# Two-layer diffusion trunk on one core: softmax weights split by ScalarE and VectorE straight from PSUM, q/k norm gains folded into the rotation tables, doubled heads written at once

## The chip, the core and the metric

The kernel runs on one core of a Trainium2 chip. The metric is the device time of one execution in microseconds, as the median over runs. Five engines work side by side, each through its own queue in order: TensorE (PE; PEld is its weight load), VectorE (DVE), ScalarE (ACT), GpSimd (POOL) and the queue from which the DMAs are issued (SP).

## The reference

Two token groups, 128 prompt tokens and 512 latent tokens, go through two layers with the same weights. What matters here is the attention part of a layer:

```
h  = rmsnorm(x, norm1) * (1 + sc1) + sh1
qa, ka, va, qb, kb, vb, uc = split(h @ w_in)
qa = rmsnorm(qa per head of 64, qn_a); ka, qb, kb alike with kn_a, qn_b, kn_b
if latent tokens: rotate qa, ka, qb, kb by cos, sin of the position; add the cached keys and values
oa: 4 heads, softmax(q1 k1 / 8) - lam * softmax(q2 k2 / 8), times va     (differential)
ob: 8 query heads over 2 key heads, softmax(q k / 8) times vb            (GQA)
oc: pooling mixer;  merged = gates * (oa, ob, oc projections);  x = x + g1 * (merged @ w_out)
```

A gated MLP follows. The normed keys (not rotated) and the values of the prompt tokens are outputs too.

## The kernel before

All tensors are float32. A matmul of full precision is made of three matmuls of fp32r operands: every operand is split into a high part (a copy rounded to fp32r) and a low part (the rest), and `mm3` adds high times low, low times high and high times high.

Each layer has an attention phase and then merge, out and MLP phases, which the change doesn't touch. The attention phase has six units in the order `order`: two GQA units (kind 1: 4 q heads and 1 k head) and four differential ones (kind 0: 2 q and 2 k heads). `unit` projects five token tiles of 128 (tile 0 is the prompt): 24 matmuls into one PSUM tile `mm` (`ps_m`, one slot), a copy to `raw` by ACT (two slots), then the norm and the rotation: `sqq` is the square by ACT, `ss` its sum per head and then mean plus eps by DVE, `rq` the power -1/2 by POOL (`powr`); `y0` is raw times the norm gain by POOL, `y` is y0 times cos by POOL, `y2` is y0 with its halves swapped times sin by two DVE instructions, POOL adds y2 to y, and two DVE instructions write y times rq into both halves of `dup`, in which each head stands twice. `transposes` turns dup on PE into `tr` (a PSUM tile), from which ACT writes the high part `qk` and DVE the low part.

A unit's attention (`tasks_gqa`, `tasks_diff`) runs while the next unit, or dense products of the pooling input (`in_u`), of gates (`gate`) and of the pooling mixer (`mix`), are projected; `weave` sets the order by cost figures, and the framework then orders instructions on each engine by a timeline of its own. Scores `sc` of 128 queries go through maximum (DVE), exponential (ACT) and scaling to the weights `w`. `pv_pair` turns the weights of two query tiles on PE into three PSUM tiles `pt` (512, 512 and 256 columns); `put_pt` splits each into `ph` and `pl`; the products with the values go to `pv`. In `put_pt` of before, ACT copies the PSUM tile to `pt` in SBUF, DVE casts that to ph, and POOL subtracts ph from it. `tr`, `pt` and `trc` (the cached keys) share a pool of two PSUM slots, `ps_t`. A PSUM slot is free again after its last reader.

GpSimd reads and writes SBUF alone here; all its instructions of the attention phase have SBUF operands.

Of the kernel before, what the change touches and what calls it, by code (L numbers as in the profile page):

```python
# [12 lines left out]
F32 = mybir.dt.float32  # L13
F32R = mybir.dt.float32r
AF = mybir.ActivationFunctionType
ALU = mybir.AluOpType
# [4 lines left out]
P = 128  # L21
# [7 lines left out]
EPS = 1e-6  # L29
# [27 lines left out]
def trunk_kernel(ctx: ExitStack, tc: tile.TileContext, a: dict):  # L57
    nc = tc.nc
    dma = nc.sync.dma_start
    vec, act, pool, pe = nc.vector, nc.scalar, nc.gpsimd, nc.tensor  # L60

    def tp(name, bufs=1, stack=None, **kw):
        return (stack or ctx).enter_context(
            tc.tile_pool(name=name, bufs=bufs, reuse_waits="tile", **kw))
# [173 lines left out]
    def attention_phase(l, hh, hl, w0):  # L238
        lam_init = 0.8 - 0.6 * math.exp(-0.3 * l)
        with ExitStack() as st:  # L240
            late = tp("late", 2, st)
            ap = tp("att", 2, st)
# [3 lines left out]
            rows = ap.tile([P, 8, 64], F32, tag="dup", name="rowv")  # L246
            dma(rows, a["rowv"][l])

            lt = ap.tile([P, 2, 64], F32, tag="sq", name="lt", bufs=5)
            lam2 = small.tile([P, 2], F32, tag="lam2", name="lam2", bufs=1)  # L250
            nlam = small.tile([P, 1], F32, tag="nlam", name="nlam", bufs=1)
            vec.tensor_tensor(out=lt[:, 0], in0=rows[:, 4], in1=rows[:, 5], op=ALU.mult)
# [3 lines left out]
            vec.tensor_tensor(out=nlam, in0=lam2[:, 1:2], in1=lam2[:, 0:1], op=ALU.subtract)  # L256
            vec.tensor_scalar_add(out=nlam, in0=nlam, scalar1=-lam_init)

            gains = []
            for kind, (nq, nk) in enumerate(((2, 2), (4, 1))):  # L260
                g = ap.tile([P, 5, 64], F32, tag=f"gain{kind}", name=f"gain{kind}", bufs=1)
                vec.tensor_scalar_mul(out=g[:, :nq], in0=rows[:, 2 * kind:2 * kind + 1].to_broadcast([P, nq, 64]),
                                      scalar1=0.125)
                vec.tensor_copy(g[:, nq:nq + nk], rows[:, 2 * kind + 1:2 * kind + 2].to_broadcast([P, nk, 64]))
                gains.append(g)
            cos = ap.tile([P, 4, 64], F32, tag="cos", name="cos", bufs=1)
            sin = ap.tile([P, 4, 64], F32, tag="sin", name="sin", bufs=1)
            dma(cos, a["cos"])
            dma(sin, a["sin"])
            subg = small.tile([P, 1], F32, tag="subg", name="subg", bufs=1)  # L270
            vec.tensor_scalar_mul(out=subg, in0=vecs[l][:, V_SL:V_SL + 1], scalar1=1.0 - lam_init)

# [18 lines left out]
            def unit(kind, idx, w, out, prefetch):  # L291

                nq, nk = (2, 2) if kind == 0 else (4, 1)
                nh = nq + nk
                g = gains[kind]
                vw = P if kind == 0 else 64
                qk = ap.tile([P, 6, 768], F32R, tag="qk", name="qk")
                v1 = ap.tile([P, 6, P], F32R, tag="v1", name="v1")
# [26 lines left out]
                ps = ps_t.tile([P, 4, P], F32, tag="p", name="trc")  # L325
                for i in range(nk):
# [3 lines left out]
                                  op=ALU.subtract)  # L330
# [4 lines left out]
                for tt in range(5):  # L335
                    ts = slice(tt * P, (tt + 1) * P)
                    ps = ps_m.tile([P, 384], F32, tag="mm", name="mm")
                    for k in range(ND):
                        hi, lo = w[k // 2]
                        ws = slice((k % 2) * 384, (k % 2) * 384 + 384)  # L340
                        mm3(ps, hh[:, k, ts], hl[:, k, ts], hi[:, ws], lo[:, ws], k == 0, k == 7)
                        yield 0.49
                    if late_tr is not None:
                        transposes(*late_tr)
                        yield 0.5
                    if tt == 3:
                        prefetch()
                    raw = ap.tile([P, 384], F32, tag="raw", name="raw")
                    act.activation(raw, ps, AF.Copy)  # L349
                    slot = 5 if tt == 0 else tt  # L350
                    put_v(raw[:, nh * 64:nh * 64 + vw], slot)
                    qkr = raw[:, :nh * 64].rearrange("p (h d) -> p h d", d=64)
                    sq = ap.tile([P, 5, 64], F32, tag="sq", name="sqq", bufs=5)
                    act.activation(sq[:, :nh], qkr, AF.Square)
                    ss = small.tile([P, 8], F32, tag="ss", name="ss")
                    vec.tensor_reduce(out=ss[:, :nh], in_=sq[:, :nh], axis=AX.X, op=ALU.add)
                    vec.tensor_scalar(out=ss[:, :nh], in0=ss[:, :nh], scalar1=1.0 / 64, scalar2=EPS,
                                      op0=ALU.mult, op1=ALU.add)
                    rr = small.tile([P, 8], F32, tag="rq", name="rq")
                    powr(rr[:, :nh], ss[:, :nh])  # L360
                    dup = ap.tile([P, 5, 2, 64], F32, tag="dup", name="dup")
                    y0 = ap.tile([P, 5, 64], F32, tag="sq", name="y0", bufs=5)
                    pool.tensor_tensor(out=y0[:, :nh], in0=qkr, in1=g[:, :nh], op=ALU.mult)
                    rb = rr[:, :nh].unsqueeze(2).to_broadcast([P, nh, 64])
                    if tt == 0:
                        for j in range(2):
                            vec.tensor_tensor(out=dup[:, :nh, j], in0=y0[:, :nh], in1=rb, op=ALU.mult)
# [6 lines left out]
                    else:  # L374
                        y = ap.tile([P, 5, 64], F32, tag="sq", name="y", bufs=5)
                        y2 = ap.tile([P, 5, 64], F32, tag="sq", name="y2", bufs=5)
                        pool.tensor_tensor(out=y[:, :nh], in0=y0[:, :nh],
                                           in1=cos[:, tt - 1:tt].to_broadcast([P, nh, 64]), op=ALU.mult)
                        for h in range(2):
                            hs = slice(32 * h, 32 * h + 32)  # L380
                            vec.tensor_tensor(out=y2[:, :nh, hs], in0=y0[:, :nh, 32 - 32 * h:64 - 32 * h],
                                              in1=sin[:, tt - 1:tt, hs].to_broadcast([P, nh, 32]), op=ALU.mult)
                        pool.tensor_tensor(out=y[:, :nh], in0=y[:, :nh], in1=y2[:, :nh], op=ALU.add)
                        for j in range(2):
                            vec.tensor_tensor(out=dup[:, :nh, j], in0=y[:, :nh], in1=rb, op=ALU.mult)
                    late_tr = (dup.rearrange("p h a d -> p h (a d)"), nh, nq, qk, slot)
                transposes(*late_tr)
                yield 0.5
# [50 lines left out]
            def put_pt(ps, n):  # L439
                ph = late.tile([P, 512], F32R, tag="ph", name="ph", bufs=3)  # L440
                pl = late.tile([P, 512], F32R, tag="pl", name="pl", bufs=2)
                st = late.tile([P, 512], F32, tag="pt", name="pt", bufs=2)[:, :n]
                act.activation(st, ps[:, :n], AF.Copy)
                vec.tensor_copy(ph[:, :n], st)  # L444
                pool.tensor_tensor(out=pl[:, :n], in0=st, in1=ph[:, :n].bitcast(F32), op=ALU.subtract)  # L445
                return ph, pl

            def pv_pair(ws, emit):
# [272 lines left out]
            for i, items in enumerate(FILL):  # L721
                made = []
                n = len(items)
# [5 lines left out]
                if i < len(order):  # L729
                    kind, idx = order[i]  # L730
# [162 lines left out]
    for c in range(2):  # L893
        ps = ps_d.tile("csp")
# [66 lines left out]
    for l in range(L):  # L961
        dst.close()
        xst.close()
        attention_phase(l, hh, hl, w0)
        w0 = None
        xst = ExitStack()
# [15 lines left out]
        with ExitStack() as ms:  # L982
# [11 lines left out]
            for gi, (f0, f1) in enumerate(GROUPS):  # L994
# [156 lines left out]
```

## Time and profile before

| what | value |
|---|---|
| median of 3 runs | 2333.85 us (2330.75 to 2335.5) |
| the profiled execution | 2329.09 us, span 2327.3 us |
| PE, DVE, ACT, POOL busy, share of the span | 96%, 70%, 42%, 32% |
| attention phase of layer 1 (first product of a unit to first gate of the merge phase) | 44.8 to 436.6 us |
| attention phase of layer 2 | 1183.2 to 1580.0 us |

The span runs from the first to the last instruction of the profile. A granted clock of 1.00 is 2.4 GHz on TensorE, 0.50 is 1.2 GHz. An engine's busy share is an average over very unlike stretches, so the rows further down are taken by stretch. A wait names the instruction that ended it.

### The profile page before, as it was taken

How to read it: one execution, taken by the hardware profiler on the slowest of the kernel's cores; microseconds unless marked ns; L12 is line 12 of the kernel's file. 1: busy time of each engine (PE TensorE's matmuls, PEld its weight loads, DVE VectorE, ACT ScalarE, POOL GpSimd, SP SyncE). 2: the span in 40 equal slices, each digit the busy share in tenths (PEclk: the TensorE clock that was granted, in tenths of full speed). 3: DMA queues.
4: the chain of work that ended last, by engine and by line, in shares of the span. 5: the costliest groups of instructions: out<-in, count | busy, mean ns of one | idle time of the engine just before them, and what ended most of it. 6: DMA issues, size and time to landing. Idle time of an engine off the chain costs nothing. (4 is left out here: it accounts for less than half of the span.)

```text
span 2327.3 us, 38124 instructions
## 1 busy us (share of the span) xinstructions
PE 2227.8 (96%) x14778; PEld 2168.6 (93%) x14778; DVE 1633.0 (70%) x2971; ACT 978.7 (42%) x1728; POOL 747.1 (32%) x835
## 2 busy tenths in 40 slices
PE   8988998999999999999988999999999999999999
PEld 4888988999999999999978988899999999999999
DVE  6888788559668757765598877965795776554555
ACT  4544555432245424332454545644323454242422
POOL 3886775215031000000058866642331300000000
PEclk8999999999999999999999999999999999999999
DMA  7211213276443333432232122224762422312123
GB/s 269 68 52 58 70 63 104 87 255 226 135 127 104 102 106 118 136 102 86 86 114 75 42 69 81 95 75 132 268 209 91 145 94 95 102 60 93 52 83 114
DMA packets 102776, 258.52 MB, mean 111 GB/s; under 512 B 19522, under 2 KB 32578, under 8 KB 102595
## 3 DMA queue, kind: packets, MB, share of 16 engines
q1 hardware_dynamic: 102596, 256.09, 33.7%
q8 instruction: 116, 1.90, 0.3%
q14 instruction: 64, 0.52, 0.1%
HBM read 233.10 MB, written 22.95 MB: 110 GB/s over the span
## 5 line engine op out<-in xcount | busy, mean ns | idle before, releaser
L96 DVE TENSOR_TENSOR wl<-st,wh 128x1024 fp32r<-128x1024 f32 (+3 forms) x336 | 388.7, 1161 | 75.5 <-ACT wh L95 74.6
L113 PE MATMUL up<-h2l,wh 128*128 128x320 f32 x1408 | 435.3, 310 | 2.4 <-DVE h2l L209 2.4
L95 ACT ACTIVATE wh<-st 128x1024 fp32r<-128x1024 f32 (+3 forms) x336 | 314.7, 943 | 291.0 <-PE dn L114 168.8
L114 PE MATMUL up<-h2h,wh 128*128 128x320 f32 x1408 | 434.9, 309 | 0.0
L112 PE MATMUL up<-h2h,wl 128*128 128x320 f32 x1408 | 432.8, 310 | 1.5 <-ACT v L851 1.4
L113 PEld LDWEIGHTS up<-h2l,wh 128*128 128x128 f32 x1408 | 264.8, 188 | 3.1 <-DVE h2l L209 3.1
L112 PEld LDWEIGHTS up<-h2h,wl 128*128 128x128 f32 x1408 | 264.0, 188 | 2.7 <-ACT v L851 1.9
L114 PEld LDWEIGHTS up<-h2h,wh 128*128 128x128 f32 x1408 | 264.8, 188 | 0.1
L143 DVE SCALAR_TENSOR_TENSOR junk<-stm,cs 128x1024 bf16<-128x1024 f32 x172 | 221.4, 1287 | 59.6 <-DMA stm<-in_w_mod 56.9
L445 POOL TENSOR_TENSOR pl<-pt,ph 128x512 fp32r<-128x512 f32 (+2 forms) x156 | 185.9, 1195 | 146.0 <-DVE ph L444 90.3
L854 DVE SCALAR_TENSOR_TENSOR v<-u,vecs,v 128x127 f32<-128x127 f32 (+1 forms) x176 | 89.0, 546 | 183.7 <-ACT v L851 183.7
L112 PE MATMUL mm<-wh,hl 128*128 128x384 f32 x480 | 169.6, 353 | 10.7 <-ACT raw L349 6.5
L113 PE MATMUL dn<-al,wh 128*128 128x320 f32 x544 | 168.1, 309 | 0.0
L114 PE MATMUL dn<-ah,wh 128*128 128x320 f32 x544 | 168.1, 309 | 0.0
L112 PE MATMUL dn<-ah,wl 128*128 128x320 f32 x544 | 168.1, 309 | 0.0
L113 PE MATMUL mm<-wl,hh 128*128 128x384 f32 x480 | 165.5, 345 | 1.5 <-DVE wl L96 1.5
L114 PE MATMUL mm<-wh,hh 128*128 128x384 f32 x480 | 164.7, 343 | 0.0
L125 POOL COPY stm<-v 128x1 f32<-128x1 f32 x32 | 27.6, 878 | 404.4 <-DVE v L856 339.8
L112 PE MATMUL gp<-hh,wl 128*128 128x320 f32 x480 | 148.4, 309 | 0.0
L114 PE MATMUL gp<-hh,wh 128*128 128x320 f32 x480 | 148.0, 308 | 0.0
L113 PE MATMUL gp<-hl,wh 128*128 128x320 f32 x480 | 148.0, 308 | 0.0
L112 PE MATMUL mmu<-hh,wl 128*128 128x384 f32 (+1 forms) x416 | 134.9, 324 | 7.1 <-ACT up L666 5.1
(227 smaller groups left out, 5787.1 us busy)
## 6 DMA issues: line engine op xcount, KB each, us to landing
stm<-in_w_mod SPq DMA_DIRECT2D x88, 512.0 KB, 4.3
st<-in_w_up SPq DMA_DIRECT2D x88, 512.0 KB, 3.6
st<-in_w_gate SPq DMA_DIRECT2D x48, 512.0 KB, 4.3
st<-in_w_unit SPq DMA_DIRECT2D x48, 384.0 KB, 3.3
st<-in_w_out SPq DMA_DIRECT2D x32, 512.0 KB, 3.7
st<-in_w_down SPq DMA_DIRECT2D x48, 320.0 KB, 2.9
st<-in_w_br SPq DMA_DIRECT2D x24, 512.0 KB, 3.6
st<-in_w_down SPq DMA_DIRECT2D x32, 384.0 KB, 3.2
```

The source lines that it names most:

```text
L95: act.activation(hi, x, AF.Copy)
L96: eng.tensor_tensor(out=lo, in0=x, in1=hi.bitcast(F32), op=ALU.subtract)
L112: pe.matmul(out, sl, mh, start=start, stop=False)
L113: pe.matmul(out, sh, ml, start=False, stop=False)
L114: pe.matmul(out, sh, mh, start=False, stop=stop)
L125: pool.tensor_copy(dst[:, 0:1], after[0])
L143: vec.scalar_tensor_tensor(out=junk, in0=st, scalar=1.0, in1=cs[:, j], op0=ALU.mult, op1=ALU.mult, accum_out=col)
L445: pool.tensor_tensor(out=pl[:, :n], in0=st, in1=ph[:, :n].bitcast(F32), op=ALU.subtract)
L854: vec.scalar_tensor_tensor(out=v[:, s + 1:e], in0=u[:, s:e - 1], scalar=cw[0], in1=v[:, s + 1:e], op0=ALU.mult, op1=ALU.add)
```

## The change

1. `put_pt`: ACT writes the high part `ph` straight from the PSUM tile, and DVE subtracts it from the same PSUM tile into `pl`. DVE's cast, POOL's subtraction and the SBUF tile `pt` are gone. The PSUM slot is now held until DVE's subtraction, and no longer until ACT's copy.
2. Norm gains: tables `cg` = gain times cos and `sg` = gain times sin are made once in a phase for each kind, for q and k apart. POOL makes `y` = raw times cg in one multiplication (two instructions in a GQA unit, 256 and 64 columns), DVE makes `y2` from raw and sg (two instructions, in a GQA unit four), so y0 is gone.
3. The square is scaled and a 65th column holds eps, so that the sum over it needs no further instruction (L357 of before is gone). The squares live in two tiles of their own.
4. One DVE instruction writes both halves of dup, for 4 or 5 heads 512 or 640 columns.
5. `cos` and `sin` are loaded into slots of the weight tiles `w`.

```diff
-            gains = []
...
+            vec.tensor_scalar_mul(out=rows[:, 0:4:2], in0=rows[:, 0:4:2], scalar1=0.125)
+            cos = late.tile([P, 4, 64], F32, tag="w", name="cos", bufs=4)
+            sin = late.tile([P, 4, 64], F32, tag="w", name="sin", bufs=4)
             dma(cos, a["cos"])
             dma(sin, a["sin"])
+            for kind in range(2):
...
+                for typ in range(2):
+                    g = rows[:, 2 * kind + typ:2 * kind + typ + 1]
+                    vec.tensor_copy(cg[:, 0:1, typ], g)
+                    vec.tensor_tensor(out=cg[:, 1:, typ], in0=cos, in1=g.to_broadcast([P, 4, 64]), op=ALU.mult)
+                    for h in range(2):
+                        hs, ho = slice(32 * h, 32 * h + 32), slice(32 - 32 * h, 64 - 32 * h)
+                        vec.tensor_tensor(out=sg[:, :, typ, hs], in0=sin[:, :, hs],
+                                          in1=g[:, :, ho].to_broadcast([P, 4, 32]), op=ALU.mult)
...
-                    act.activation(sq[:, :nh], qkr, AF.Square)
+                    act.activation(sq[:, :nh, :64], qkr, AF.Square, scale=0.125)
...
-                    vec.tensor_scalar(out=ss[:, :nh], in0=ss[:, :nh], scalar1=1.0 / 64, scalar2=EPS,
-                                      op0=ALU.mult, op1=ALU.add)
...
+                    for of, by in zip(parts, gain):
+                        pool.tensor_tensor(out=of(y), in0=of(qkr), in1=by(cg[:, tt]), op=ALU.mult)
                     powr(rr[:, :nh], ss[:, :nh])
-                    pool.tensor_tensor(out=y0[:, :nh], in0=qkr, in1=g[:, :nh], op=ALU.mult)
...
+                    vec.tensor_tensor(out=dup[:, :nh], in0=y[:, :nh].unsqueeze(2).to_broadcast([P, nh, 2, 64]),
+                                      in1=rr[:, :nh].unsqueeze(2).unsqueeze(2).to_broadcast([P, nh, 2, 64]),
+                                      op=ALU.mult)
...
-                        pool.tensor_tensor(out=y[:, :nh], in0=y0[:, :nh],
-                                           in1=cos[:, tt - 1:tt].to_broadcast([P, nh, 64]), op=ALU.mult)
...
-                        for j in range(2):
-                            vec.tensor_tensor(out=dup[:, :nh, j], in0=y[:, :nh], in1=rb, op=ALU.mult)
...
-                act.activation(st, ps[:, :n], AF.Copy)
-                vec.tensor_copy(ph[:, :n], st)
-                pool.tensor_tensor(out=pl[:, :n], in0=st, in1=ph[:, :n].bitcast(F32), op=ALU.subtract)
+                act.activation(ph[:, :n], ps[:, :n], AF.Copy)
+                vec.tensor_tensor(out=pl[:, :n], in0=ps[:, :n], in1=ph[:, :n].bitcast(F32), op=ALU.subtract)
```

In the kernel after, lines of this part stand 11 or 12 further down (L445 of before is L456).

POOL's queue in layer 1, where the attention of the first GQA unit runs beside the first `in_u` (the windowed sums are `win`). Before:

```order
L445 TENSOR_TENSOR pl<-pt,ph 128x256
L445 TENSOR_TENSOR pl<-pt,ph 128x512 x2
L673 TENSOR_TENSOR win<-up 128x663
L436 TENSOR_SCALAR w<-w,rs 128x640
L673 TENSOR_TENSOR win<-win 128x661
L436 TENSOR_SCALAR w<-w,rs 128x640
L673 TENSOR_TENSOR win<-win 128x657
L445 TENSOR_TENSOR pl<-pt,ph 128x256
L445 TENSOR_TENSOR pl<-pt,ph 128x512
L673 TENSOR_TENSOR win<-win 128x649
```

And now:

```order
L449 TENSOR_SCALAR w<-w,rs 128x640 x4
L684 TENSOR_TENSOR win<-up 128x663
L118 TENSOR_TENSOR rq<-ss,mhalf 128x4
L684 TENSOR_TENSOR win<-win 128x661
L684 TENSOR_TENSOR win<-win 128x657
L684 TENSOR_TENSOR win<-win 128x649
```

The subtractions have left POOL's queue, and the scalings of w and the powers rq stand closer together. DVE's queue at the same place now holds them; before:

```order
L385 TENSOR_TENSOR dup<-y,rq 128x4x64 x2
L444 CAST ph<-pt 128x512
L284 TENSOR_TENSOR qk<-tr,qk 64x2x128
L288 TENSOR_TENSOR qk<-tr,qk 128x2x128
L96 TENSOR_TENSOR wl<-st,wh 128x768
L527 TENSOR_TENSOR ob_836<-pv,ob_836 64x256
```

And now:

```order
L389 TENSOR_TENSOR dup<-y,rq 128x512
L96 TENSOR_TENSOR wl<-st,wh 128x768
L445 TENSOR_REDUCE nm<-sc 128x1
L296 TENSOR_TENSOR qk<-tr,qk 64x2x128
L300 TENSOR_TENSOR qk<-tr,qk 128x2x128
L456 TENSOR_TENSOR pl<-pt,ph 128x256
L456 TENSOR_TENSOR pl<-pt,ph 128x512
L538 TENSOR_TENSOR ob_845<-pv,ob_845 64x256
```

Where a cast stood, a subtraction from PSUM stands, and dup takes one instruction. The third place is the start of a phase. In SP's queue the tables' loads stood right behind the load of the gains; before:

```order
L247 DMA rowv<-in_rowv 128x512
L268 DMA cos<-in_cos 128x256
L269 DMA sin<-in_sin 128x256
L318 DMA ck<-in_cache_gqa_k 128x64 x2
```

And now they stand behind the store of the first unit's prompt keys:

```order
L397 DMA out_new_gqa_k<-dup 128x64
L262 DMA cos<-in_cos 128x256
L263 DMA sin<-in_sin 128x256
L102 DMA st<-in_w_u 128x1024 x3
```

By the program they wait there for an instruction of DVE as well. DVE's queue after the third token tile's sum ss, now:

```order
L368 TENSOR_REDUCE ss<-sqe_494 128x5
L322 CAST v_502<-v_501 128x64
L271 TENSOR_TENSOR cg_474<-cos,rowv 128x4x64 x2
L271 TENSOR_TENSOR cg_484<-cos,rowv 128x4x64 x2
L274 TENSOR_TENSOR sg_475<-sin,rowv 128x4x32 x4
L274 TENSOR_TENSOR sg_485<-sin,rowv 128x4x32 x4
L386 TENSOR_TENSOR y_610<-raw,sg_485 128x4x32
L386 TENSOR_TENSOR y_668<-raw,sg_485 128x4x32
```

Twelve instructions that make the tables stand ahead of the first rotation (y2, printed y_610 and y_668) of token tiles 1 and 2; before, tile 1's rotation stood ahead of tile 2's sum.

## Rows read from the trace of the kernel before

**Rows 1.** Engine busy time by stretch; PEclk is the granted clock.

```profile
core 0: us, PE busy (x) PEld busy (x) DVE busy (x) ACT busy (x) POOL busy (x), PEclk, DMA share, GB/s
44.80:70.00 25.20, 20.52 (x93) 18.40 (x94) 25.08 (x72) 14.70 (x31) 14.12 (x22) 0.84 0.35 100
70.00:436.60 366.60, 336.99 (x2197) 323.84 (x2196) 296.13 (x607) 192.52 (x439) 255.06 (x292) 0.97 0.22 72
1183.20:1215.00 31.80, 24.79 (x123) 20.12 (x123) 30.92 (x89) 16.70 (x45) 15.11 (x25) 0.94 0.21 68
1215.00:1580.00 365.00, 332.68 (x2169) 319.28 (x2169) 291.10 (x595) 190.74 (x429) 250.99 (x289) 0.97 0.22 72
760.00:1120.00 360.00, 360.00 (x2457) 360.00 (x2456) 230.91 (x396) 124.72 (x160) 16.78 (x22) 1.00 0.33 106
```

**Rows 2.** What PE waited for, 70 to 436.6 us: total, times, longest.

```profile
PE tr L280 <- DVE dup L385: 6.2, 4, 3.4
PE pv L579 <- POOL pl L445: 2.9, 2, 1.5
...
PE poolp L112 <- ACT oc L653: 0.2, 1, 0.2
```

**Rows 3.** The same from 1215 to 1580 us.

```profile
PE tr L280 <- DVE dup L385: 5.0, 3, 3.4
...
PE pv L113 <- POOL pl L445: 0.2, 1, 0.2
...
```

**Rows 4.** PE in order of time: start, us, instruction, idle before.

```profile
133.43 0.60 PE L456 MATMUL pt<-ident,w 128*128 128x128 f32 x4
135.48 0.39 PE L579 MATMUL pv<-pl,v 128*128 128x256 f32 x1 [1.46 <-POOL pl L445]
```

**Rows 5.** The longest waits of all engines, 44.8 to 436.6 us.

```profile
POOL pl L445 <- DVE ph L444: 38.8, 24, 8.9
...
ACT pt L443 <- POOL pl L445: 18.1, 12, 4.8
```

**Rows 6.** DVE groups by shape, 44.8 to 436.6 us: busy, mean ns, idle before.

```profile
L444 DVE CAST ph<-pt 128x512 fp32r<-128x512 f32 x46 | 29.5, 645 | 11.8 <-PE pv L580 5.7 <-ACT pt L443 4.7 <-ACT z L635 1.1
...
L96 DVE TENSOR_TENSOR wl<-st,wh 128x1024 fp32r<-128x1024 f32 x16 | 23.9, 1500 | 4.3 <-ACT wh L95 4.2
L385 DVE TENSOR_TENSOR dup<-y,rq 128x256 f32<-128x256 f32 x32 | 23.2, 764 | 3.9 <-POOL y L383 1.8 <-POOL rq L118 1.6 <-PE tr L280 0.3
...
L444 DVE CAST ph<-pt 128x256 fp32r<-128x256 f32 x22 | 11.6, 527 | 4.2 <-ACT pt L443 2.1 <-PE pv L580 1.1 <-PE pv L562 0.8
L385 DVE TENSOR_TENSOR dup<-y,rq 128x320 f32<-128x320 f32 x16 | 8.9, 592 | 0.6 <-POOL rq L118 0.5
...
L288 DVE TENSOR_TENSOR qk<-tr,qk 128x256 fp32r<-128x256 f32 x20 | 8.5, 424 | 0.3
...
L284 DVE TENSOR_TENSOR qk<-tr,qk 64x512 fp32r<-64x512 f32 x10 | 6.9, 694 | 2.7 <-ACT qk L281 2.5
...
L357 DVE TENSOR_SCALAR ss<-ss 128x4 f32<-128x4 f32 x20 | 6.2, 311 | 0.1
```

**Rows 7.** DVE in order of time: start, us, instruction.

```profile
99.90 0.41 DVE L444 CAST ph<-pt 128x512 fp32r<-128x512 f32 x1
```

**Rows 8.** POOL groups by shape, 44.8 to 436.6 us.

```profile
L445 POOL TENSOR_TENSOR pl<-pt,ph 128x512 fp32r<-128x512 f32 x46 | 64.7, 1410 | 36.9 <-DVE ph L444 28.8 <-PE pv L113 2.7 <-PE pv L580 1.3
...
L445 POOL TENSOR_TENSOR pl<-pt,ph 128x256 fp32r<-128x256 f32 x22 | 18.8, 857 | 13.4 <-DVE ph L444 7.6 <-PE pv L579 2.9 <-PE pv L580 1.4
...
L377 POOL TENSOR_TENSOR y<-y,cos 128x256 f32<-128x256 f32 x16 | 13.6, 852 | 0.0
```

**Rows 9.** DVE groups by shape from 760 to 1120 us, where POOL is almost idle.

```profile
L96 DVE TENSOR_TENSOR wl<-st,wh 128x1024 fp32r<-128x1024 f32 x34 | 41.5, 1221 | 0.0
```

**Rows 10.** DVE in order of time: the last reader of x.

```profile
66.28 0.47 DVE L206 SCALAR_TENSOR_TENSOR ht<-x,A,bc 128x256 f32<-128x256 f32 x1
```

**Rows 11.** DMA issues: count, KB each, us from issue to landing.

```profile
cos<-in_cos SPq DMA_DIRECT2D x2, 128.0 KB, 3.5
```

More of the change, by code (lines that the diff above doesn't have):

```diff
@@ L247, in attention_phase @@
             dma(rows, a["rowv"][l])
-            lt = ap.tile([P, 2, 64], F32, tag="sq", name="lt", bufs=5)
+            lt = ap.tile([P, 2, 64], F32, tag="sq", name="lt", bufs=4)
             lam2 = small.tile([P, 2], F32, tag="lam2", name="lam2", bufs=1)
@@ L257, in attention_phase @@
             vec.tensor_scalar_add(out=nlam, in0=nlam, scalar1=-lam_init)
-            gains = []
[L260 to L267, printed above, removed]
+            vec.tensor_scalar_mul(out=rows[:, 0:4:2], in0=rows[:, 0:4:2], scalar1=0.125)
+            cos = late.tile([P, 4, 64], F32, tag="w", name="cos", bufs=4)
+            sin = late.tile([P, 4, 64], F32, tag="w", name="sin", bufs=4)
             dma(cos, a["cos"])
             dma(sin, a["sin"])
+            cgs, sgs = [], []
+            for kind in range(2):
+                cg = ap.tile([P, 5, 2, 64], F32, tag=f"cg{kind}", name=f"cg{kind}", bufs=1)
+                sg = ap.tile([P, 4, 2, 64], F32, tag=f"sg{kind}", name=f"sg{kind}", bufs=1)
+                for typ in range(2):
[6 more added lines that the diff above has]
+                                          in1=g[:, :, ho].to_broadcast([P, 4, 32]), op=ALU.mult)
+                cgs.append(cg)
+                sgs.append(sg)
+            sqs = [ap.tile([P, 5, 65], F32, tag=f"sqe{i}", name=f"sqe{i}", bufs=1) for i in range(2)]
+            for q in sqs:
+                vec.memset(q[:, :, 64:65], EPS)
             subg = small.tile([P, 1], F32, tag="subg", name="subg", bufs=1)
@@ L294, in unit @@
                 nh = nq + nk
-                g = gains[kind]
+                cg, sg = cgs[kind], sgs[kind]
                 vw = P if kind == 0 else 64
@@ L352, in unit @@
                     qkr = raw[:, :nh * 64].rearrange("p (h d) -> p h d", d=64)
-                    sq = ap.tile([P, 5, 64], F32, tag="sq", name="sqq", bufs=5)
-                    act.activation(sq[:, :nh], qkr, AF.Square)
+                    sq = sqs[tt % 2]
+                    act.activation(sq[:, :nh, :64], qkr, AF.Square, scale=0.125)
                     ss = small.tile([P, 8], F32, tag="ss", name="ss")
                     vec.tensor_reduce(out=ss[:, :nh], in_=sq[:, :nh], axis=AX.X, op=ALU.add)
-                    vec.tensor_scalar(out=ss[:, :nh], in0=ss[:, :nh], scalar1=1.0 / 64, scalar2=EPS,
-                                      op0=ALU.mult, op1=ALU.add)
@@ L359, in unit @@
                     rr = small.tile([P, 8], F32, tag="rq", name="rq")
-                    powr(rr[:, :nh], ss[:, :nh])
-                    dup = ap.tile([P, 5, 2, 64], F32, tag="dup", name="dup")
-                    y0 = ap.tile([P, 5, 64], F32, tag="sq", name="y0", bufs=5)
-                    pool.tensor_tensor(out=y0[:, :nh], in0=qkr, in1=g[:, :nh], op=ALU.mult)
-                    rb = rr[:, :nh].unsqueeze(2).to_broadcast([P, nh, 64])
+                    dup = ap.tile([P, 5, 2, 64], F32, tag="dup", name="dup")
@@ new lines, in unit @@
+                    y = ap.tile([P, 5, 64], F32, tag="sq", name="y", bufs=4)
+                    if kind == 0:
+                        parts = [lambda t: t[:, :4].rearrange("p (a h) d -> p a h d", a=2)]
+                        gain = [lambda t: t.unsqueeze(2).to_broadcast([P, 2, 2, t.shape[2]])]
+                    else:
+                        parts = [lambda t: t[:, :4], lambda t: t[:, 4:5]]
+                        gain = [lambda t: t[:, 0:1].to_broadcast([P, 4, t.shape[2]]), lambda t: t[:, 1:2]]
@@ new lines, in unit @@
+                    for of, by in zip(parts, gain):
+                        pool.tensor_tensor(out=of(y), in0=of(qkr), in1=by(cg[:, tt]), op=ALU.mult)
+                    powr(rr[:, :nh], ss[:, :nh])
+                    if tt > 0:
+                        y2 = ap.tile([P, 5, 64], F32, tag="sq", name="y2", bufs=4)
+                        for h in range(2):
+                            hs = slice(32 * h, 32 * h + 32)
+                            for of, by in zip(parts, gain):
+                                vec.tensor_tensor(out=of(y2[:, :, hs]), in0=of(qkr[:, :, 32 - 32 * h:64 - 32 * h]),
+                                                  in1=by(sg[:, tt - 1, :, hs]), op=ALU.mult)
+                        pool.tensor_tensor(out=y[:, :nh], in0=y[:, :nh], in1=y2[:, :nh], op=ALU.add)
@@ L365, in unit @@
+                    vec.tensor_tensor(out=dup[:, :nh], in0=y[:, :nh].unsqueeze(2).to_broadcast([P, nh, 2, 64]),
+                                      in1=rr[:, :nh].unsqueeze(2).unsqueeze(2).to_broadcast([P, nh, 2, 64]),
+                                      op=ALU.mult)
                     if tt == 0:
-                        for j in range(2):
-                            vec.tensor_tensor(out=dup[:, :nh, j], in0=y0[:, :nh], in1=rb, op=ALU.mult)
                         if kind == 0:
@@ L373, in unit @@
                             dma(a["new_gqa_v"][l, :, idx], raw[:, 320:384])
-                    else:
-                        y = ap.tile([P, 5, 64], F32, tag="sq", name="y", bufs=5)
-                        y2 = ap.tile([P, 5, 64], F32, tag="sq", name="y2", bufs=5)
-                        pool.tensor_tensor(out=y[:, :nh], in0=y0[:, :nh],
-                                           in1=cos[:, tt - 1:tt].to_broadcast([P, nh, 64]), op=ALU.mult)
[L379 to L384, printed above, removed]
-                            vec.tensor_tensor(out=dup[:, :nh, j], in0=y[:, :nh], in1=rb, op=ALU.mult)
                     late_tr = (dup.rearrange("p h a d -> p h (a d)"), nh, nq, qk, slot)
@@ L441, in put_pt @@
                 pl = late.tile([P, 512], F32R, tag="pl", name="pl", bufs=2)
-                st = late.tile([P, 512], F32, tag="pt", name="pt", bufs=2)[:, :n]
-                act.activation(st, ps[:, :n], AF.Copy)
-                vec.tensor_copy(ph[:, :n], st)
-                pool.tensor_tensor(out=pl[:, :n], in0=st, in1=ph[:, :n].bitcast(F32), op=ALU.subtract)
+                act.activation(ph[:, :n], ps[:, :n], AF.Copy)
+                vec.tensor_tensor(out=pl[:, :n], in0=ps[:, :n], in1=ph[:, :n].bitcast(F32), op=ALU.subtract)
                 return ph, pl
```

## The prediction

> **What bounds the kernel now.** Read first where TensorE is short of work. From 760 to 1120 us, in the MLP, it is busy all the time at a granted clock of 1.00; the change can give nothing there. In the two attention phases it is not [rows 1]. Each has a start (44.8 to 70 and 1183.2 to 1215 us) in which DVE is busy for 25.1 of 25.2 and 30.9 of 31.8 us with norms and modulation that the change leaves alone. What follows, 366.6 and 365 us, is where the change works: PE is busy 337.0 and 332.7 us, so it idles 29.6 and 32.3 us, 62 us together, and its mean granted clock is 0.97, a mix of the levels 2.4 and 1.2 GHz, so a further 0.03 x 366 = 11 us in each phase, 22 us, is the most that the slow level costs. DVE is busy for 80%, POOL for 69%, ACT for 52% of these stretches.
>
> Then the waits of PE. The list of the first phase has 22 lines that sum to 29 us, that of the second 23 lines with 33 us [rows 2, 3]; shown are the first rows of each and one from its end. I sorted the whole lists by releaser: DVE or POOL ended 20.4 and 23.1 us, 43.5 together, ACT the other 19. Of the 43.5, dup before its transposes is 11.2 (6.2 and 5.0), the low part pl before the value products 5.7, and 26.6 are late instructions of DVE (the folding of ob, scalings, the low parts of qk, ph).
>
> One place in order of time shows how such a wait looks: transposes start at 133.43 and the next product at 135.48, 2.05 us later; 1.46 is shown as a wait for pl [rows 4]. Four transposes need some 0.35 us back to back, so about 0.25 us more is lost that counts as busy. The two lists count 68 waits, hence about 17 us that no idle time shows.
>
> Last, why pl is late. POOL waited 38.8 us, 24 times, for DVE's cast, and ACT 18.1 us for POOL to free an SBUF tile pt [rows 5]: three engines in a row, each with a queue, stand between transposes and products.
>
> **The change part by part, for one phase.** DVE first. Gone are the casts, 29.5 + 11.6 us, the pairs of dup, 23.2 + 8.9 us and for the prompt tile 12 more at 0.59, 7 us, and thirty small instructions L357 at 0.31 (ten of them GQA's), 9.3 us [rows 6]: 89.5 us. The subtraction from PSUM has no row of its own; the nearest are the low parts of qk, which also take one operand from PSUM and one from SBUF: 0.694 us for 512 columns, 0.424 for 256 [rows 6]. So pl costs 46 x 0.694 + 22 x 0.424 = 41.2 us, as much as the casts. dup in one write: 20 x 0.694 and, scaled by 640/512, 10 x 0.87, 22.6 us. GQA's two further y2 instructions, 16 at no more than 0.31, cost 5 us, and the tables, 19 instructions at about that price, 6 us. Added: 75 us; net 15 us less.
>
> The price of the casts hangs on their company: the mean is 0.645, but one took 0.41 [rows 7]. The Trainium skill (VectorE: DVE Perf Modes, section Mode 2×_2P) says that a copy within SBUF can run two elements per cycle and a two-input operation cannot, which speaks against trading the one for the other. By 0.41 the casts would be 18.9 instead of 29.5 us and DVE would gain 4 us and not 15; the means, which include the waiting, are what the phase paid, and I go by them.
>
> POOL loses pl, 64.7 + 18.8 us, and 24 products with cos at 0.85, 20 us, and gains ten small ones, about 4 us [rows 8]: 99 of 269 us, so its share falls from 69 to about 43%. That helps DVE in turn. The split of a 128x1024 weight takes 1.50 us in the phase [rows 6] and 1.22 where POOL is idle [rows 9]. On 47 us of DVE instructions of this kind (the weight splits and the new dup) the excess is about 9 us, and 37% less POOL gives back 3 to 4; with the kinds left out I take 5. DVE: 20 us less in each phase, 321 to about 301.
>
> In the Trainium skill (SBUF — State Buffer, section Who interferes with whom) an instruction of DVE with two SBUF inputs contends with GpSimd and one with a single SBUF input does not. The rows agree: 0.764 for dup of 256 columns with both inputs in SBUF, 0.424 for qk of 256 with one in PSUM.
>
> Now what PE gets. The waits for pl, 5.7 us, go with POOL's part of that chain. The chain to dup loses the L357 step, one of two dup writes and the place of rq behind 1.4 us of pl: three quarters of 11.2, 8.4 us. For the other 26.6 us the bounds are nothing and all; with POOL 37% and DVE 6% less busy and a step less in the chain I take half, 13 us. The 19 us that ACT ends stay. Together 27 us. Of the 17 hidden us half go too, 8, and of the 22 us of the slow clock, which comes behind such gaps, half, 11 (bounds 0 to all for both). Gain: 46 us.
>
> Against that, two costs. At the start the tables' loads now wait for DVE, I take it for the last reading of x, which ends at 66.75 us in the first phase [rows 10]; with 3.5 us to landing [rows 11] and two issues the tables begin at 71 us and end, 12 instructions at 0.3 to 0.42, at 75. The first rotation comes at 76. Behind it wait the two slots of raw, and behind them ACT's copy of the fourth token tile and PE's projection of the fifth. Slots and the tile in work hide part of these 9 us; I take a third as a wait of PE, 3 us in each phase, 6 us, with the bounds 0 and 18. SP's queue holds behind these loads weights of later products alone. Squares, memsets and copies of gains lie under the start's own DVE work and the projection.
>
> The other is the PSUM slot. A pt tile is now held until DVE has subtracted, and transposes of the next but one tile wait for that. 46 tiles of a phase (tr and trc) are read by DVE already; waits of PE for them sum to 7.9 us over both phases (lines with qk in the lists of [rows 2, 3]), 0.09 us a tile. 156 pt tiles at that price are 13 us, a little less with a quicker DVE: 10 us. The upper bound is what POOL bore of DVE's lateness, 38.8 us a phase [rows 5], 78 us.
>
> Sum: 46 - 6 - 10 = 30 us less. The profiled execution took 2329.1 us (span 2327.3, 1.8 us around it); 2299. The median of the runs lies 4.8 us above it: 2304.
>
> **The rivals.** First, the queues nearly empty: if a third less POOL and shorter chains end almost all waits of DVE and POOL, 43.5 + 17 + 22 - 6, some 76 us, could be had; four fifths of it, 61, gives 2273. For it speaks that ACT, the third engine, is at 52%; against it that DVE stays at 75%.
>
> Second, the relief is off the path: POOL's and DVE's time falls, but PE's waits shift to ACT and to the order of instructions, which has been made anew on all engines. Then half of the gain comes, 23 us, and the costs of 16 stand: 2327, between 2319 and 2339. The low price of an undisturbed cast speaks for it.
>
> Third, slower: the PSUM slots pace PE. The three pt tiles of a pair need a third slot while the first is held, and dup's tr tiles want the same two. If 0.7 of the 78 us falls on PE, the costs are 60 against 46: 2348; it decides from half of the 78 upward. Against it: DVE no longer waits for POOL, and the newly made order puts other products between pt tiles in most places.
>
> That the change does not do what it says can be left out: the new order shows pl in DVE's queue and none in POOL's.
>
> **How the numbers follow.** Chances: the forecast (2290 to 2322 us) 0.50, the emptied queues 0.15, off the path 0.20, the slots 0.15. Less than 0.2%, 4.7 us, can hardly be told from no change by three runs of this kernel; of the off-path case 0.09 lies within it and 0.11 below. So faster 0.76, same 0.09, slower 0.15. The range reaches from the middle of the first rival to just above the second: 2266 to 2342, which leaves out most of the third and a part of the first.
>
> **What would show it.** Right: pl on DVE at about 0.69 and 0.42 us; POOL at some 170 us in a phase and DVE near 300; the lists of PE's waits without pl behind POOL, with dup at a few us; PE's idle time in each long stretch nearer 18 than 31 us. Wrong: new lines in which pt or tr wait for DVE's pl, of more than 5 us a phase; a gap at the fifth token tile of several us at each start; or idle time of PE as before with ACT as its releaser. The prediction fails on the fast side if pl and dup get cheaper than their rows, and on the slow side if the slots cost more than 0.2 us a tile.

## The result, and the profile after

| | before | after |
|---|---|---|
| median (runs) | 2332.3 us (2325.97 to 2335.5, 4) | 2301.66 us (2299.74 to 2307.55, 4) |
| ratio, 95% interval | | 0.9876 (0.9848 to 0.9904) |
| the profiled execution | 2329.09 us, span 2327.3 | 2307.55 us, span 2305.3 |

The change takes 30.6 us off, and the predicted 2304 lies 2.3 us above the median. The profiled execution of after is the slowest of its four. The kernel was run and profiled once more beside the last experiments: 2301.84 us (2295.57 to 2304.22, 4 runs), and its two attention phases took 376.1 and 382.7 us against 376.4 and 382.2 here. So the phases are read from this profile, and most of what it has too much lies between them (750.6 us from 425.4 to 1176, 747.2 in the second profile, 746.6 before).

The attention phases run from 49.0 to 425.4 and from 1176.0 to 1558.2 us. The view of busy time by stretch of the kernel after, cut where [rows 1] is cut, at the first token tiles and behind them:

```profile
core 0: us, PE busy (x) PEld busy (x) DVE busy (x) ACT busy (x) POOL busy (x), PEclk, DMA share, GB/s
49.00:74.00 25.00, 20.73 (x109) 19.19 (x109) 24.68 (x76) 13.85 (x28) 12.82 (x22) 0.94 0.33 97
74.00:425.40 351.40, 332.12 (x2206) 319.02 (x2205) 262.84 (x571) 191.66 (x441) 153.48 (x206) 0.99 0.23 75
1176.00:1208.00 32.00, 22.95 (x118) 18.51 (x118) 30.87 (x98) 15.59 (x41) 13.68 (x25) 1.00 0.22 68
1208.00:1558.20 350.20, 333.02 (x2196) 320.26 (x2197) 259.43 (x557) 190.46 (x434) 152.22 (x204) 0.98 0.23 75
```

Against [rows 1]: PE idles 19.3 and 17.2 us in the long stretches, 36.5 for 61.9 before; DVE is busy for 74 to 75% and no longer 80%, POOL for 44% and no longer 69%, and the granted clock is 0.99 and 0.98 where it was 0.97 twice.

What PE waited for from 74 to 425.4 us (total, times, longest), which answers to [rows 2]:

```profile
PE pt L467 <- DVE pl L456: 2.9, 3, 1.8
PE pt L495 <- DVE qk L296: 2.8, 1, 2.8
PE mm L112 <- ACT raw L361: 2.2, 2, 2.0
PE pv L112 <- ACT ph L455: 1.7, 2, 1.5
PE sc L419 <- ACT e L428: 1.4, 1, 1.4
...
PE tr L292 <- DVE pl L456: 0.8, 1, 0.8
```

And from 1208 to 1558.2 us, for [rows 3]:

```profile
PE mm L112 <- ACT raw L361: 5.0, 3, 4.1
PE pt L467 <- DVE pl L456: 3.3, 4, 1.8
PE pt L495 <- DVE qk L296: 2.8, 1, 2.8
...
```

No line of either list names POOL, and none names dup. New are the first line of the one list and the second of the other: a transpose waits until DVE has subtracted and the slot of the pool `ps_t` is free.

DVE's groups by shape, 49 to 425.4 us (busy, mean ns, idle before), for [rows 6]:

```profile
L456 DVE TENSOR_TENSOR pl<-pt,ph 128x512 fp32r<-128x512 f32 x46 | 31.2, 682 | 6.4 <-ACT ph L455 6.2
L96 DVE TENSOR_TENSOR wl<-st,wh 128x1024 fp32r<-128x1024 f32 x16 | 20.9, 1305 | 3.7 <-ACT wh L95 3.7
L386 DVE TENSOR_TENSOR y<-raw,sg 128x128 f32<-128x128 f32 x48 | 18.3, 409 | 5.2 <-ACT raw L361 5.2
L389 DVE TENSOR_TENSOR dup<-y,rq 128x512 f32<-128x512 f32 x20 | 14.9, 745 | 6.1 <-POOL rq L118 4.5 <-PE tr L292 1.5
L389 DVE TENSOR_TENSOR dup<-y,rq 128x640 f32<-128x640 f32 x10 | 9.4, 937 | 4.0 <-POOL rq L118 3.6 <-POOL y L388 0.3
L456 DVE TENSOR_TENSOR pl<-pt,ph 128x256 fp32r<-128x256 f32 x22 | 9.2, 417 | 3.3 <-PE pv L590 2.0 <-ACT ph L455 0.5
```

The subtraction from PSUM costs what its nearest row said, 0.682 and 0.417 us where 0.694 and 0.424 were taken. POOL's first group in the same stretch, where [rows 8] had pl:

```profile
L449 POOL TENSOR_SCALAR w<-w,rs 128x640 f32<-128x640 f32 x32 | 29.4, 920 | 63.0 <-DVE rs L448 62.3 <-PE pv L590 0.3 <-DMA d<-o_dram 0.3
```

POOL now stands idle for 62.3 us ahead of its scalings, waiting for DVE's reciprocal rs, where before it waited 9.0 us: at this place its queue is mostly empty.

At the start, ACT, PE and DVE in order of time (start, us, instruction, idle before):

```profile
69.63 0.47 ACT L366 ACTIVATE sqe<-raw 128x320 f32<-128x320 f32 x1
76.38 0.49 ACT L361 ACTIVATE raw<-mm 128x384 f32<-128x384 f32 x1 [6.28 <-DVE y L386]
```

```profile
76.92 0.45 PE L112 MATMUL mm<-wh,hl 128*128 128x384 f32 x1 [2.02 <-ACT raw L361]
```

```profile
75.07 1.29 DVE L386 TENSOR_TENSOR y<-raw,sg 128x128 f32<-128x128 f32 x8
```

ACT has no slot of raw until the first rotations (DVE's y from sg, at 75.07) have read it, as the prediction drew it; PE's share of these 6.3 us is 2.0.

### The profile page after: what moved, and what is told of

The parts are those of the page before. It is cut to its first block, busy times and chain, and to the rows that moved or that the text cites. A ratio compares the mean times of both kernels' runs of the same rounds, so it can differ in the third digit from the quotient of the medians.

```text
span 2305.3 us, 37922 instructions
## 1 busy us (share of the span) xinstructions
PE 2225.9 (97%) x14778; PEld 2163.6 (94%) x14778; DVE 1562.8 (68%) x2913; ACT 975.7 (42%) x1728; POOL 528.4 (23%) x651
## 5 line engine op out<-in xcount | busy, mean ns | idle before, releaser
L96 DVE TENSOR_TENSOR wl<-st,wh 128x1024 fp32r<-128x1024 f32 (+3 forms) x336 | 375.4, 1120 | 71.7 <-ACT wh L95 71.1
L114 PE MATMUL mmu<-hh,wh 128*128 128x384 f32 (+1 forms) x416 | 131.0, 315 | 0.0
L113 PE MATMUL mmu<-hl,wh 128*128 128x384 f32 (+1 forms) x416 | 130.4, 314 | 0.0
```

The costliest lines, as they stand in the source:

```text
L96: eng.tensor_tensor(out=lo, in0=x, in1=hi.bitcast(F32), op=ALU.subtract)
```

## The experiments

Each version's instructions are put in order anew by the framework, so that a small difference between two versions can be one of order and not of cost. "Before" is the median of the runs of the kernel before on the same chip: 2331.32 us beside e1, e4, e5 and e6, 2329.45 beside e3, e7, e8 and e9, 2333.83 beside e10 to e13. The phases below are from busy time by stretch, from the first product of a unit to the first gate of the merge, the two summed; PE idle is their length less PE's busy time.

| version | median us (runs) | ratio to before, 95% | phases us | PE idle | DVE / POOL busy |
|---|---|---|---|---|---|
| before | | | 788.6 | 73.6 | 643 / 535 |
| after | 2301.66 (4) | 0.9876 (0.9848 to 0.9904) | 758.6 | 49.8 | 578 / 332 |
| e1 split only | 2306.6 (4) | 0.9901 (0.9884 to 0.9917) | 765.7 | 59.4 | 602 / 365 |
| e4 slot held, old chain | 2345.99 (4) | 1.0071 (1.0056 to 1.0086) | 800.2 | 86.6 | 634 / 527 |
| e5 split, POOL loaded | 2320.94 (5) | 0.9959 (0.9944 to 0.9973) | 782.3 | 68.5 | 612 / 501 |
| e6 slot freed early | 2324.52 (7) | 0.9971 (0.996 to 0.9982) | 772.3 | 61.2 | 611 / 382 |
| e7 split, fold, dup | 2299.26 (4) | 0.9866 (0.9848 to 0.9883) | 758.1 | 47.9 | 585 / 360 |
| e12 the same again | 2300.73 (4) | 0.9863 (0.9845 to 0.9881) | 758.2 | 48.3 | 584 / 363 |
| e3 tables early | 2299.65 (4) | 0.9863 (0.9845 to 0.9882) | 758.0 | 46.7 | 581 / 330 |
| e11 the same again | 2300.31 (4) | 0.9863 (0.9841 to 0.9884) | 756.3 | 46.7 | 581 / 331 |
| e10 after again | 2301.84 (4) | 0.9863 (0.984 to 0.9886) | 758.8 | 49.9 | 578 / 328 |
| e8 scaling on DVE | 2305.24 (4) | 0.9891 (0.9874 to 0.9909) | 763.9 | 49.6 | 616 / 277 |
| e13 scaling on ACT | 2304.92 (4) | 0.9882 (0.9863 to 0.99) | 761.8 | 54.8 | 576 / 273 |
| e9 weight splits on POOL | 2322.34 (9) | 0.9964 (0.9951 to 0.9976) | 766.5 | 54.7 | 577 / 389 |

**e1: of the change, the split of the softmax weights alone**, in the kernel before.

```diff
-                act.activation(st, ps[:, :n], AF.Copy)
-                vec.tensor_copy(ph[:, :n], st)
-                pool.tensor_tensor(out=pl[:, :n], in0=st, in1=ph[:, :n].bitcast(F32), op=ALU.subtract)
+                act.activation(ph[:, :n], ps[:, :n], AF.Copy)
+                vec.tensor_tensor(out=pl[:, :n], in0=ps[:, :n], in1=ph[:, :n].bitcast(F32), op=ALU.subtract)
```

> Only the split of the weights is changed (ACT writes ph from PSUM, DVE subtracts from PSUM); norm, rotation and dup as before. Theory (POOL and one step leave the chain from transposes to products): most of the whole change's 30 us, 18 to 25 us under before, no PE wait for pl behind POOL, new waits of pt for DVE's pl of about 5 us a phase. Rival (the gain is DVE's saved work in norm, rotation and dup): under 10 us, since pl costs DVE what the cast cost.

24.7 us less than before (2331.32): four fifths of the whole. Norm, rotation and dup are here as before. Transposes wait 3.8 and 6.1 us in the two phases for DVE's pl, near the 5 expected.

**e4: the slot held until DVE has read it, in the old chain.** DVE casts ph from the PSUM tile; POOL's subtraction and the SBUF copy stay.

```diff
-                vec.tensor_copy(ph[:, :n], st)
+                vec.tensor_copy(ph[:, :n], ps[:, :n])
```

> Before, with one operand changed: DVE casts ph from the PSUM tile and not from ACT's copy, so the PSUM slot is held until DVE has read it, and the chain over POOL stays. The cast is then about 0.69 us and alone on its port. Theory (0.09 us a tile): 8 to 14 us slower than before. Rival (the slots pace PE, most of the 78 us of DVE's lateness shows): 30 us slower or more. A third: no difference, the slots are free in time anyway.

14.7 us more than before. PE's longest wait by total from 44 to 440 us is the held slot, a line that [rows 2] does not have:

```profile
PE pt L456 <- DVE ph L444: 5.2, 6, 2.2
```

And from 1192.3 to 1596.7 us, in the second phase:

```profile
PE pt L456 <- DVE ph L444: 6.0, 6, 2.2
```

PE idles 13.0 us more than before in the two phases, and 11.2 of them are these waits. So holding a slot costs time in the way that the forecast drew. What it costs beside the new chain this run does not say; there the waits for pl are to be read.

**e5: the split with POOL loaded as before.** To e1 a subtraction on POOL is added that reads ph and writes a tile that nobody reads.

```diff
+                pj = late.tile([P, 512], F32, tag="pt", name="pj", bufs=2)
+                pool.tensor_tensor(out=pj[:, :n], in0=ph[:, :n].bitcast(F32), in1=ph[:, :n].bitcast(F32), op=ALU.subtract)
```

> The split as in the run with the split alone, but POOL does a subtraction of the same size from ph into a tile that nobody reads, so its work stays that of before while it is out of the chain. Theory (the chain counts): within 6 us of the split alone. Rival (POOL's load counts, through its queue for the scalings of w and rq and through DVE's port): 12 to 20 us slower than the split alone, near before.

10.4 us less than before, 14.3 more than e1. So the shorter chain, with POOL out of it but still busy (501 us for 535), is worth some 10 us, and the other 14 hang on POOL's work. POOL's groups by shape, 46 to 425 us, with the dummy and the scalings of w:

```profile
L445 POOL TENSOR_TENSOR pj<-ph 128x512 f32<-128x512 f32 x46 | 50.5, 1107 | 40.4 <-ACT ph L442 40.4
L436 POOL TENSOR_SCALAR w<-w,rs 128x640 f32<-128x640 f32 x32 | 31.1, 975 | 6.5 <-DVE rs L435 5.6 <-DVE ss L357 0.9
```

The same scalings in e1, 46 to 425 us:

```profile
L436 POOL TENSOR_SCALAR w<-w,rs 128x640 f32<-128x640 f32 x32 | 28.9, 907 | 36.4 <-DVE rs L435 34.5 <-DVE ss L357 1.7
```

POOL waits for DVE's rs ahead of them only 5.6 us, against 34.5 in e1 and 62.3 in after: they now stand in line behind other work, the dummy too. By what path that reaches PE is not shown. Of PE's waits only 0.5 us, in the second phase, name POOL's w. Those for the low parts of qk, for ACT's z and w and for DVE's rs grew by 4 to 6 us each from e1, and DVE's busy time rose from 602 to 612 us. Two DVE groups in e5, 46 to 425 and 48.8 to 437.9 us, the subtraction and the weight splits:

```profile
L443 DVE TENSOR_TENSOR pl<-pt,ph 128x512 fp32r<-128x512 f32 x46 | 31.3, 683 | 13.1 <-ACT ph L442 10.0 <-PE pv L561 3.0
L96 DVE TENSOR_TENSOR wl<-st,wh 128x1024 fp32r<-128x1024 f32 x16 | 20.8, 1301 | 2.2 <-ACT wh L95 2.2
```

The subtraction takes 0.683 us whether POOL is loaded or not (0.682 in after). The split, with both inputs in SBUF, takes 1.301 us with POOL busy for 65% of the phase, no more than the 1.305 of after at 44%.

**e6: the slot freed early.** ACT copies the tile to SBUF, makes ph from that copy, and DVE subtracts within SBUF.

```diff
                 act.activation(st, ps[:, :n], AF.Copy)
-                vec.tensor_copy(ph[:, :n], st)
-                pool.tensor_tensor(out=pl[:, :n], in0=st, in1=ph[:, :n].bitcast(F32), op=ALU.subtract)
+                act.activation(ph[:, :n], st, AF.Copy)
+                vec.tensor_tensor(out=pl[:, :n], in0=st, in1=ph[:, :n].bitcast(F32), op=ALU.subtract)
```

> The split alone, but ACT copies the PSUM tile to SBUF first, rounds ph from that copy, and DVE subtracts both from SBUF: the PSUM slot is free after ACT's first copy, for one more ACT instruction of 0.4 to 0.6 us a tile (some 40 us of ACT in a phase) and a subtraction with two SBUF operands. If the held slot costs PE 10 us or more, this is 5 us or more faster than the split alone; if it costs little, slower than it by 5 to 15 us.

17.9 us slower than e1. The slots are no longer held, but DVE's subtraction with both operands in SBUF is dearer, and ACT is busy for 477 us of the two phases and not 413:

```profile
L445 DVE TENSOR_TENSOR pl<-pt,ph 128x512 fp32r<-128x512 f32 x46 | 36.2, 791 | 5.1 <-PE pv L579 2.9 <-ACT ph L444 2.1
```

Of the difference 6.6 us lie within the phases; the rest lies outside them in its profile (752.7 us between them for e1's 744.6), at least partly where ACT is late at the border of the merge phase. So this does not price the slot; it says that freeing it in this way is no bargain.

**e7 and e12: split, eps in the sum and dup in one write**, the rotation as before. e1's edit and:

```diff
...
-                    act.activation(sq[:, :nh], qkr, AF.Square)
+                    act.activation(sq[:, :nh, :64], qkr, AF.Square, scale=0.125)
...
-                    vec.tensor_scalar(out=ss[:, :nh], in0=ss[:, :nh], scalar1=1.0 / 64, scalar2=EPS,
-                                      op0=ALU.mult, op1=ALU.add)
...
-                        for j in range(2):
-                            vec.tensor_tensor(out=dup[:, :nh, j], in0=y[:, :nh], in1=rb, op=ALU.mult)
+                        vec.tensor_tensor(out=dup[:, :nh], in0=y[:, :nh].unsqueeze(2).to_broadcast([P, nh, 2, 64]),
+                                          in1=rr[:, :nh].unsqueeze(2).unsqueeze(2).to_broadcast([P, nh, 2, 64]),
+                                          op=ALU.mult)
```

> The split alone, and in addition eps folded into the sum (no L357) and dup written once; gains and rotation by y0 and cos as before. It takes 26 us of DVE's prices (dup 39 to 23, L357 9) out of each phase and makes no tables. Theory: 6 to 10 us under the split alone, near 2299, so under after by 1 to 3 us since the start's 6 us are not paid. Rival (these instructions are off the path once POOL is): within 3 us of the split alone, 2307.

> The kernel before with the new put_pt, eps in the sum and dup in one write, with the rotation in its old form (POOL makes y0 and y, no tables of products). If the gain tables are worth what they take off POOL (13 to 16 us of busy time in a phase against this kernel), this one is 2 to 5 us slower than the version with early tables. If POOL is off the path once pl has left it, the two are alike within 1 us, about 2298, and the gain tables give nothing.

Ratios 0.9866 and 0.9863 against e1's 0.9901: some 8 us more. With that the whole of the gain is there, without gain tables. Which of the two edits gives the 8 us no run shows.

**e3 and e11: the changed kernel with its tables early.** cos and sin lie in SBUF tiles of their own tag and are loaded ahead of the first unit.

```diff
-            cos = late.tile([P, 4, 64], F32, tag="w", name="cos", bufs=4)
-            sin = late.tile([P, 4, 64], F32, tag="w", name="sin", bufs=4)
+            cos = ap.tile([P, 4, 64], F32, tag="sq", name="cos", bufs=4)
+            sin = ap.tile([P, 4, 64], F32, tag="sq", name="sin", bufs=4)
```

> After, with one change: cos and sin are loaded into slots that are free at the start (those of y and y2), so the tables are made among the start's own work and not behind the last reading of x. Theory (the start costs PE 2.0 and 4.1 us, seen as waits for raw behind y2): 4 to 6 us under after, about 2297, and no wait of ACT's raw for DVE's y2 over 2 us. Rival (DVE is busy all through the start, so the 4 us of tables only move in front of the normed inputs that PE waits for): no difference from after, within 2 us.

> The changed kernel itself, beside the two versions that follow, on one chip and with more runs, since 0.1% is in question. Theory: the tables' late loads cost the start 6 us, so this kernel is 3 to 6 us slower than the one with early tables (about 2301.5 against 2297). Rival: the wait at the start is taken back later, and the two are alike within 1 us.

> The changed kernel with cos and sin in SBUF tiles of their own tag, loaded early. In its first profile PE's waits for raw in the two starts are 4.3 us against 9.6 in the changed kernel. Theory: 3 to 6 us under the changed kernel, about 2297. Rival: alike within 1 us.

The wait goes. PE's waits in the first start of e11 (46 to 80 us), where the changed kernel has 4.3 us, the longest of 2.0:

```profile
PE mm L112 <- ACT raw L361: 1.7, 3, 0.6
```

In the second start 2.3 us stand against 5.3. That is 5.6 us less of this wait in e11, while the waits for wl and hl in the two starts grew by 2.0; PE's idle time falls by 3.1 us, the phases by 0.6 to 2.5, and the median by 1.5 to 2, which is within the scatter. So the start's wait is there at its forecast size, and other waits take most of it back. Versions with the tables (e11) and without them (e12) agree within 0.4 us although POOL is busy for 32 us less with them: the folding of the gains, with what its tables cost, gives nothing that can be measured.

**e8 and e13: the scaling of GQA's weights w moved from POOL**, to DVE in the changed kernel (e8), to ACT in the version with early tables (e13).

```diff
-                pool.tensor_scalar(out=w, in0=w, scalar1=rs[:, 0:1], scalar2=1.0, op0=ALU.mult, op1=ALU.mult)
+                vec.tensor_scalar_mul(out=w, in0=w, scalar1=rs[:, 0:1])        (e8)
+                act.activation(w, w, AF.Copy, scale=rs[:, 0:1])                (e13)
```

> After, with GQA's scaling of the weights w by DVE in place of POOL: 32 instructions a phase, POOL 29 us less, DVE 18 us more at 0.58 us each. If POOL's place in the chain is what PE still pays (the run with POOL loaded was 14 us slower than the split alone): 5 to 10 us under after. If DVE's queue is the bound now (PE's waits name DVE in 10 to 15 us a phase): 5 to 10 us over after.

> The version with early tables, and the scaling of GQA's weights w by 1/sum made by ACT where POOL made it (32 instructions of 0.92 us in a phase leave POOL, about 0.8 us each come to ACT, 26 us). Theory that the queues between transposes and products set the waits: the chain exponential, sum, scaling, transpose loses an engine of slow instructions, but ACT, which has to release mm and pt, gets 13% more work; the two about cancel, within 3 us of the version with early tables. Rival, ACT is the next bound (it ends some 8 us of PE's waits in a phase): 6 to 12 us slower. Other rival, POOL's queue still counts: 4 to 8 us faster, about 2292, and best of all.

Both medians are 3 to 5 us above those of the kernels that they change, with overlapping intervals. Some 28 of POOL's 166 us a phase were taken away, and that is worth no more than what it costs on DVE or on ACT; relief of POOL alone these two runs do not price. The scaling itself is quicker on DVE, 0.584 us for 640 columns where POOL needs 0.920 and ACT 0.837, and it still does not pay.

**e9: low parts of weights on POOL.** In the changed kernel POOL makes the low part wl of 13 of the 16 weights of 128x1024 in a phase.

```diff
-load_w(a["w_u" if kind == "u" else "w_gate"][l, n], 1024)
+load_w(a["w_u" if kind == "u" else "w_gate"][l, n], 1024, pool)
```

> After, with the low parts of the pooling-input and gate weights of the attention phase made by POOL: DVE 21 us less a phase, POOL some 30 to 40 us more, in pieces of 2 us and more. If DVE's queue is the bound: 5 to 10 us under after. If POOL's load and its place in the chain count, as the run with POOL loaded says: 3 to 10 us over after.

20.7 us slower than after by the medians, more than either theory had. POOL and DVE groups by shape, 46 to 425 and 48 to 429 us:

```profile
L96 POOL TENSOR_TENSOR wl<-st,wh 128x1024 fp32r<-128x1024 f32 x13 | 31.9, 2460 | 11.7 <-ACT wh L95 11.7
...
L386 DVE TENSOR_TENSOR y<-raw,sg 128x128 f32<-128x128 f32 x48 | 21.8, 481 | 8.5 <-ACT raw L361 8.5
L389 DVE TENSOR_TENSOR dup<-y,rq 128x512 f32<-128x512 f32 x20 | 16.7, 837 | 8.6 <-PE tr L292 5.1 <-POOL rq L118 3.5
```

13 splits of 1.305 us, 17 us, left DVE in the first phase, and its busy time there went from 287.5 to 286.0: what stayed got slower, y2 of 128 columns from 0.409 to 0.481 and dup from 0.745 to 0.837 us. The phases are 7.7 us longer than in the second profile of after; its profile is the fastest of its nine runs and shows some 6 us more outside the phases. The rest of the 20 stays open.

## Why the prediction was right, point by point

**The sum.** The phases were to get 30 us shorter, and they did: 788.6 to 758.6. Its parts lie otherwise. Forecast were 27 us of waits gained less 16 of new ones, so 11 of idle time, and 19 of losses that no idle time shows and of the slow clock. Idle time fell by 23.8 and PE's busy time by 6.2. The first term was too small and the second too large, by about 13 us each, so that the sum came out within 2 us is in part luck. The cut between the two is soft: the profile of before has 45 matmul records fewer in the phases than that of after, at the mean of 0.15 us up to 7 us that count as idle there.

**Waits gained, term 27, measured 41.** The 5.7 us behind POOL's pl are gone, as forecast. Of dup's 11.2, all are gone and not three quarters. DVE's other waits fell from 26.6 to 10.7 (qk, ob, rs, wl), by 16 and not 13. The forecast let ACT's 19 us stay. The lists after have 17.2, but 6.1 of them are the new wait at the starts, counted below: the old ones fell to 11, by 8, and this the forecast had at nothing. With new waits of 16 (7.8, 2.4 and 6.1 below, 16 forecast) that makes 25 us, the fall of idle time in the two long stretches (61.9 to 36.5).

**Slow clock and hidden losses, term 19, measured 6.** The bound on what the slow level costs fell from 22 to 3.5 + 7 = 10.5 us, half, as taken; but this was the most that it can cost, and the measured fall of PE's busy time leaves room for no more than 6, or 13 with the missing records. Here the size was wrong: the bound was treated as a cost.

**Cost of the slots, term 10, measured 7.8.** Transposes (pt and tr) wait 3.7 and 4.1 us for DVE's pl, under the 5 us a phase that would have spoken against the forecast. Products that wait for pl add 2.4. In e4, beside the old chain, the hold cost more, 14.7 us; why it costs less here is not shown. The third rival, in which the slots pace PE, did not come about.

**Cost of the start, term 6, measured 6.1 as a wait** (2.0 and 4.1 us), and at most 2 us as time, by e3 and e11.

**Engines.** DVE was to fall from 321 to 301 us and fell to 287 and 290; POOL to 170, and fell to 166. DVE gained more than the sum had, and not by the new instructions: pl cost 40.4 us of the first phase, as forecast, and the new dup took 0.745 and not 0.694. Instructions that the change leaves alone got cheaper by more than the 5 us taken: weight splits of 768 and 1024 columns by 6.7 us in the first phase (1.50 to 1.305 for 1024), the small additions to `win` by 4.5 (6.0 to 1.5). The Trainium skill (SBUF — State Buffer, section Who interferes with whom) says that an instruction of DVE with two SBUF inputs contends with GpSimd's reads, and that one with at most one SBUF input, outside DVE's two-port modes, does not. The runs agree on both sides: the subtraction from PSUM took 0.682 to 0.684 us in after, e1, e5 and e9, with POOL busy for 166 to 253 us of a phase, while with both inputs in SBUF it took 0.791 (e6), and y2 and dup got dearer by 18% and 12% in e9, where POOL had 30 us more. The prediction left out the condition on the modes, and it scaled the price of the splits by POOL's busy share: e5, with 1.301 us at 65%, does not bear that scaling out.

**Which part gave it.** The prediction did not split its sum by edit. e1 puts some 25 us on the split, e7 and e12 another 8 on eps and dup, and the gain tables, with what they cost the start, come out at nothing. Within the split, e5 puts 10 us on the shorter chain and 14 on POOL's relief. The second rival, in which the relief is off the path, is refuted by that: more load on POOL costs time. Yet the next 32 us off POOL (e11 against e12, with DVE's busy time 3 us apart) give nothing, and in e8 and e13 no more than they cost elsewhere, so the gain from POOL ended about where pl had left it. Why the first third of POOL's load counts and these 32 us do not is read from POOL's idle time before w, 5.6 us in e5, 34.5 in e1, 62.3 in after: argued from these rows, not shown by a run of its own.

No version beats the changed kernel by more than the scatter; e11 and e12 are alike with it, and e12 gets there with three of the five edits.

## What to carry to other kernels

Before an engine's relief is priced, look at whether its queue is full where its results are waited for: much idle time in front of its instructions is a sign, in this case borne out once (e11 against e12), that further relief is worth little. When a list of waits is compared with that of before, take the new waits out of each releaser's sum first, or a gain hides behind them, as ACT's 8 us did here. A subtraction that reads PSUM on DVE can replace a cast in SBUF and a subtraction elsewhere at the cast's price, and what it costs is the longer hold of the PSUM slot, to be read from waits of PE for tiles that DVE already reads. A wait that a change adds at one place can be made up behind it, so undo the wait in a run of its own before working around it.

## What the runs showed of the hardware

DVE's instructions with two operands in SBUF vary with what POOL does beside them: the split of 128x1024 took 1.50 us in before, where POOL was busy for 69%, 1.305 at 44% in after, and 1.22 where POOL was almost idle [rows 6, 9]. POOL's busy share alone does not set the price: in e5 it was 1.301 at 65%. Moving such work from DVE to POOL freed nothing: 17 us went, and DVE's busy time stayed within 2 us (e9), while POOL took 2.46 us for what DVE does in 1.3. The subtraction of 512 columns with one operand in PSUM stayed at 0.682 to 0.684 us whatever POOL did (e1, e5, e9 and after), and so did e4's cast from PSUM, 0.682.
